# A hybrid decoder layer on one core: the last layer norm without GpSimd, four of its eight tiles finished by TensorE through a diagonal matrix

## The chip, the cores and the metric

The kernel runs on one core of a Trainium2 chip. A core has five engines that each work through a queue of their own in order: TensorE (PE; the loading of its weights is PEld), VectorE (DVE), ScalarE (ACT), GpSimd (POOL) and SyncE (SP), which here issues most of the DMA transfers. The metric is the device time of one execution in microseconds (us), and less is better.

## What is computed

One post-norm decoder layer over 1024 positions of width 1024: a token mixer in two head groups, a first layer norm, and a hierarchical mixture of experts (one of 4 groups, then 2 of its 8 experts per token). The change touches only what follows the experts, the second layer norm with its scale `ln2_g` and bias `ln2_b`:

```python
x = _layernorm(ALPHA * x + (1.0 + g2[:, None, :]) * m, ln2_g[l], ln2_b[l])

def _layernorm(x, g, b):
    mu = jnp.mean(xf, axis=-1, keepdims=True)
    var = jnp.mean(jnp.square(xf - mu), axis=-1, keepdims=True)
    y = (xf - mu) * lax.rsqrt(var + LN_EPS) * g + b
```

Everything is float32.

## The kernel before

The layer runs in stages: input projection, recurrence and gating, output projection with the first layer norm and the routing, and then the 32 experts one after the other. Each expert's result rows are added by an indirect DMA (`scatter`, line 1415) into `xad`, a table of 1024 rows in device memory that already holds `ALPHA * x`. After the last scatter has landed the **tail** begins, and all of the change lies there.

The tail works on eight tiles of 128 rows by 1024 columns. Lines 1545 and 1546 load all eight from `xad` through SP's queue; the buffers `rt` are ring buffers of the experts' weights, which the profile calls y0a, y0b, y1a and uu (two tiles each). `l2g` and `l2b`, broadcast over the 128 partitions, were loaded during the last experts (profile: vn).

`t_ops(tt)` (line 1550) returns the list of operations of tile `tt`. Two strings choose their form. `TSTAT` chooses the statistics: with "V", VectorE takes `bn_stats` over both halves (line 1556) and `bn_aggr` (1587), and ScalarE the square root (1559); with "S", ScalarE sums the row with an accumulator (1589), VectorE turns the sum into the negative mean (1590), ScalarE sums the squares around it (1591) and takes the root (1559). Then VectorE takes the reciprocal (1593), so that `sd` holds one over the deviation and `mu` the mean or its negative.

`TMODE` chooses the rest. With "F" VectorE does it in two fused operations over the tile: (r - mu) * g (line 1574), then r * sd + b (line 1572). With any other letter VectorE makes the shift in one column (1563, 1565), ScalarE normalises the tile in one pass (1598), and then come a plain multiplication by g and a plain addition of b (1570): both on GpSimd with "p", the multiplication on GpSimd and the addition on VectorE with "A", the other way round with "B". At the end SP stores the tile (1584; for tile 7 in two halves, 1582).

No scheduler orders the tail: the string `TORDER` (line 55) does, one digit for each operation, and lines 1602 and 1603 issue the next operation of that tile. As each engine takes its own instructions in that order, so do SP's stores:

```python
TSTAT = "VVVSVSVS"
TMODE = "pFBpFAFF"
TORDER = "00100102101213023231320425323423564546436567545653776777575"
...
    t_all = [t_ops(tt) for tt in range(8)]
    for tt in TORDER:
        run(t_all[int(tt)], 1)
```

So before, tiles 0 and 3 are multiplied and biased by GpSimd, tiles 2 and 5 by GpSimd and VectorE, and tiles 1, 4, 6 and 7 by VectorE alone. Also used by the change: `ident` (line 207), the 128x128 identity; `ones` (209); `eh`, made with the experts' buffers, a buffer of four 128x128 blocks that held the transposed hidden rows of an expert; and `pup`, `pup2`, `pdn` (line 1294), three PSUM buffers of two banks (profile: up, ov, dn), into which the experts' products went.

Of the kernel before, what the change touches and what calls it, by code (L numbers as in the profile page):

```python
# [15 lines left out]
AF = mybir.ActivationFunctionType  # L16
OP = mybir.AluOpType
# [6 lines left out]
P = 128  # L24
T = 1024
D = 1024
# [23 lines left out]
WE = 0  # L50
WV = ()
TB = 1
TSTAT = "VVVSVSVS"
TMODE = "pFBpFAFF"
TORDER = "00100102101213023231320425323423564546436567545653776777575"
BACC = dict(dynamic_dma_scratch_size=7168)
COLS = [slice(0, 512), slice(512, 1024)]

# [2 lines left out]
def tile_hybrid_moe_layer(  # L61
# [7 lines left out]
    nc = tc.nc  # L69
    V, S, G, PE = nc.vector, nc.scalar, nc.gpsimd, nc.tensor  # L70
# [11 lines left out]
    start = ExitStack()  # L82
# [10 lines left out]
    def cst(shape, dt, name):  # L93
        return const.tile(shape, dt, name=name)
# [112 lines left out]
    ident = cst([P, P], F32, "ident")  # L207
    V.tensor_scalar(ident, jp, 0.0, None, op0=OP.is_equal)
    ones = cst([P, P], F32, "ones")
# [36 lines left out]
    def h_turn(half, k):  # L246
        p = sm()
        for i in range(4):
            PE.transpose(p[:, i * P:(i + 1) * P], x_tile(half, k)[:, i], ident)
        return p  # L250
# [402 lines left out]
    for k in range(8):  # L653
        p = h_turn(0, k)
# [383 lines left out]
    def run(ops, m=None):  # L1038
        for _ in range(len(ops) if m is None else min(m, len(ops))):
            ops.pop(0)()  # L1040
# [205 lines left out]
    eh, eh2 = (p4.tile([P, 4, P], F32, name=n) for n in ("eh", "eh2"))  # L1246
# [47 lines left out]
    pup, pup2, pdn = (ps4.tile([P, 2, 512], F32, name=t) for t in ("up", "ov", "dn"))  # L1294
# [248 lines left out]
    l2g, l2b = l2  # L1543
# [6 lines left out]
    def t_ops(tt):  # L1550
        r, mode = rt[tt], TMODE[tt]
        mu, sd = mv8[:, tt, 0:1], mv8[:, tt, 1:2]

        def moments():
            for n, sl in enumerate(COLS):
                V.bn_stats(st8[:, tt, n], r[:, sl])

        def root(scale=1.0):
            S.activation(sd, sd, AF.Sqrt, bias=eps, scale=scale)

        def shift():
            if TSTAT[tt] == "V":
                V.scalar_tensor_tensor(mu, mu, -1.0, sd, op0=OP.mult, op1=OP.mult)
            else:
                V.tensor_tensor(mu, mu, sd, op=OP.mult)

        def part(q, sl, fused, e):
            v = (l2g, l2b)[q]
            if not fused:
                e.tensor_tensor(r[:, sl], r[:, sl], v[:, sl], op=(OP.mult, OP.add)[q])  # L1570
            elif q:
                V.scalar_tensor_tensor(r[:, sl], r[:, sl], sd, v[:, sl], op0=OP.mult, op1=OP.add)  # L1572
            else:
                V.scalar_tensor_tensor(r[:, sl], r[:, sl], mu, v[:, sl],  # L1574
                                       op0=OP.subtract if TSTAT[tt] == "V" else OP.add, op1=OP.mult)

        def both(q):
            e = {"p": (G, G), "F": (V, V), "A": (G, V), "B": (V, G), "X": (V, V), "q": (G, G)}[mode][q]
            for sl in COLS if tt == 7 else [slice(0, D)]:
                part(q, sl, mode == "F", e)  # L1580
                if q and tt == 7:
                    nc.sync.dma_start(out[0, tt * P:(tt + 1) * P, sl], r[:, sl])
            if q and tt < 7:
                nc.sync.dma_start(out[0, tt * P:(tt + 1) * P, :], r)

        if TSTAT[tt] == "V":
            ops = [moments, lambda: V.bn_aggr(mv8[:, tt], st8[:, tt]), root]
        else:
            ops = [lambda: S.activation(eyo[0], r, AF.Copy, accum_out=mu),
                   lambda: V.tensor_scalar(mu, mu, -1.0 / D, None, op0=OP.mult),  # L1590
                   lambda: S.activation(eyo[0], r, AF.Square, bias=mu, accum_out=sd),
                   lambda: root(1.0 / D)]
        ops.append(lambda: V.reciprocal(sd, sd))
        if mode == "q":
            ops.append(lambda: V.tensor_scalar(r, r, mu, sd, op0=OP.subtract if TSTAT[tt] == "V" else OP.add,
                                               op1=OP.mult))
        elif mode != "F":
            ops += [shift, lambda: S.activation(r, r, AF.Identity, bias=mu, scale=sd)]
        return ops + [lambda: both(0), lambda: both(1)]

    t_all = [t_ops(tt) for tt in range(8)]
    for tt in TORDER:
        run(t_all[int(tt)], 1)
# [23 lines left out]
```

## Time and profile before

| | |
|---|---|
| time, median of 3 runs | 1179.51 us (1179.1 to 1180.15) |
| time of the profiled execution | 1183.11 us |
| its span, first to last instruction | 1181.4 us |
| TensorE busy over the span | 88% |
| VectorE, ScalarE, GpSimd busy | 47%, 25%, 30% |
| mean granted clock of TensorE | 0.947 |

Times in the profile count from the start of the span. The granted clock is TensorE's, as a share of 2.4 GHz: it is 1.00 or 0.50 (1.2 GHz). A row of the timeline has start, duration, engine, line, operation, output and input, with the shape; "x2" are two like instructions merged, and brackets hold the idle time of the engine just before and what ended it. A row of the windows has the stretch and its length, the busy time of PE, PEld, DVE, ACT and POOL with the count of instructions in brackets, the granted clock, the share of the DMA engines that was busy and the GB/s moved. A row of the groups has line, engine, operation, output and input, shape and count, then busy us and the mean ns of one, then idle time before them.

### The profile page before, as it was taken

The page shows a single profiled execution, that of the slowest core. Times are in us where ns is not written, and L with a number is a line of the kernel's source. Part 1 is how long each engine was busy: PE and PEld are TensorE (multiplying, and loading weights), DVE is VectorE, ACT ScalarE, POOL GpSimd, SP SyncE. Part 2 cuts the span into 40 slices and gives each one's busy share as a digit, 9 for nine tenths or more (in the row PEclk, how much of TensorE's full clock was granted, in tenths as well). Part 3 has the DMA queues.
Part 4 walks back from the last instruction along what each step waited for, and adds up shares of the span by engine and source line. Part 5 has one row for each costly group of instructions (what it writes and reads, how often), then busy time and mean ns, then how long its engine had stood idle before and what let it go on. Part 6 is the DMA issues. An engine that isn't in the chain of part 4 may idle for free. (4 is left out here: it accounts for less than half of the span.)

```text
span 1181.4 us, 17353 instructions
## 1 busy us (share of the span) xinstructions
PE 1042.4 (88%) x5758; PEld 678.4 (57%) x5758; DVE 553.6 (47%) x1018; ACT 291.6 (25%) x440; POOL 359.6 (30%) x272
## 2 busy tenths in 40 slices
PE   4999999899999989998588899999998998799930
PEld 3778888788788767776333454445433553344400
DVE  6858975738664389999410211311221121211238
ACT  3363336642234442121200110101110110110113
POOL 2325643353121145552511211321141113211215
PEclk9899999999999998999799999999998998999975
DMA  9854454343211336316899979999999999999964
GB/s 278 241 164 146 143 178 144 124 157 130 89 54 54 143 143 220 120 72 248 303 393 383 351 254 371 363 386 390 371 379 395 393 371 372 394 398 384 378 247 187
DMA packets 121282, 304.55 MB, mean 258 GB/s; under 512 B 17840, under 2 KB 45144, under 8 KB 121132
## 3 DMA queue, kind: packets, MB, share of 16 engines
q1 hardware_dynamic: 111548, 275.53, 64.1%
q0 software_dynamic: 8368, 22.90, 7.2%
q10 hardware_dynamic: 1216, 4.21, 0.9%
q8 instruction: 83, 1.36, 0.5%
q14 instruction: 67, 0.55, 0.1%
HBM read 281.09 MB, written 22.88 MB: 257 GB/s over the span
## 5 line engine op out<-in xcount | busy, mean ns | idle before, releaser
L1395 DVE TENSOR_TENSOR act<-up,act 128x512 f32<-128x512 f32 x32 | 22.1, 692 | 311.6 <-ACT act L1394 234.1
L1416 POOL DMA_INDIRECT xad<-yo,tokp x36 | 52.8, 1466 | 228.4 <-DVE yo L1412 141.5
L1412 DVE SCALAR_TENSOR_TENSOR yo<-dn,wr,g2p 32x256 f32<-32x256 f32 (+2 forms) x94 | 52.1, 563 | 127.4 <-PE ov L1348 49.3
L1401 ACT ACTIVATE eh<-tp 128x512 f32<-128x512 f32 x36 | 21.1, 596 | 311.3 <-PE tp L1400 268.5
L1207 POOL DMA_INDIRECT KS<-h2d,tokp x32 | 30.5, 954 | 191.5 <-PE tp L1311 182.8
L622 PE MATMUL acc<-whi,hTh 128*128 128x512 f32 x192 | 83.0, 433 | 0.0
L166 ACT ACTIVATE whi<-wr 128x1024 fp32r<-128x1024 f32 (+1 forms) x44 | 44.9, 1021 | 128.3 <-PE acc L624 67.0
L624 PE MATMUL acc<-whi,hTl 128*128 128x512 f32 x192 | 75.9, 396 | 0.0
L623 PE MATMUL acc<-wlo,hTh 128*128 128x512 f32 x192 | 75.4, 392 | 0.0
L167 POOL TENSOR_TENSOR wlo<-wr,whi 128x1024 fp32r<-128x1024 f32 (+1 forms) x15 | 35.8, 2384 | 119.4 <-ACT whi L166 112.6
L1343 PE MATMUL up<-pring,ext 128*32 128x256 f32 (+1 forms) x564 | 53.4, 439 | 13.5 <-DMA pring<-in_w_up 10.7
L302 PEld LDWEIGHTS sm<-QP,KS 128*128 128x128 f32 x448 | 58.2, 192 | 7.3 <-issue 3.2
L618 PE MATMUL acc<-hTh,whi 128*128 128x512 f32 x144 | 59.2, 411 | 0.0
L302 PE MATMUL sm<-QP,KS 128*128 128x64 f32 x448 | 56.1, 269 | 2.6 <-DVE KS L315 1.6
L620 PE MATMUL acc<-hTh,wlo 128*128 128x512 f32 x144 | 56.9, 395 | 0.5 <-POOL wlo L167 0.2
L619 PE MATMUL acc<-hTl,whi 128*128 128x512 f32 x144 | 56.6, 393 | 0.0
L1336 PE MATMUL up<-pring,ext 128*128 128x512 f32 x128 | 56.6, 592 | 0.0
L877 PE MATMUL pa<-wh,yl 128*128 128x512 f32 (+1 forms) x128 | 51.8, 405 | 4.7 <-DVE yl L861 4.7
L876 PE MATMUL pa<-wl,yh 128*128 128x512 f32 (+1 forms) x128 | 51.6, 403 | 4.7 <-DVE wl L1048 4.7
L1394 ACT ACTIVATE act<-up 128x512 f32<-128x512 f32 x32 | 19.1, 597 | 144.4 <-PE ov L1336 52.3
L875 PE MATMUL pa<-wh,yh 128*128 128x512 f32 (+1 forms) x128 | 53.6, 419 | 1.3 <-ACT wh L1047 0.9
L443 POOL TENSOR_TENSOR vec<-vec,y1a 128x1024 f32<-128x1024 f32 x14 | 35.8, 2560 | 55.2 <-ACT y1a L442 55.2
(493 smaller groups left out, 2225.2 us busy)
## 6 DMA issues: line engine op xcount, KB each, us to landing
pring<-in_w_up SPq DMA_DIRECT2D x112, 512.0 KB
pring<-in_w_down SPq DMA_DIRECT2D x58, 512.0 KB
wr<-in_w_in SPq DMA_DIRECT2D x44, 512.0 KB
ring<-in_w_up SPq DMA_DIRECT2D x42, 512.0 KB
y1a<-in_w_ada SPq DMA_DIRECT2D x32, 512.0 KB
ring<-in_w_down SPq DMA_DIRECT2D x18, 512.0 KB
y0a<-in_w_up SPq DMA_DIRECT2D x16, 512.0 KB
y0b<-in_w_up SPq DMA_DIRECT2D x16, 512.0 KB
```

Of the source, the lines that this page charges most:

```text
L302: PE.matmul(p[:, hd], chd(KS)[:, c4, hd], chd(QP)[:, c4, hd].rearrange("p (b two i) -> p b two i", two=2, i=h)[:, :, 1, :], start=True, st ...
L618: PE.matmul(a[i], hi[:, j, sl], hTh[k], start=st, stop=False)
L619: PE.matmul(a[i], hi[:, j, sl], hTl[k], start=False, stop=False)
L620: PE.matmul(a[i], lo[:, j, sl], hTh[k], start=False, stop=sp)
L622: PE.matmul(a[i], hTh[k][:, sl], hi[:, j], start=st, stop=False)
L623: PE.matmul(a[i], hTh[k][:, sl], lo[:, j], start=False, stop=False)
L624: PE.matmul(a[i], hTl[k][:, sl], hi[:, j], start=False, stop=sp)
L875: PE.matmul(p, yh[:, k], wh[k][:, sl], start=k == 0, stop=False)
L1336: PE.matmul(p[:, h], x[:, k], gate_up(w[k], 2, h), start=k == 0, stop=k == 7)
L1343: PE.matmul(o[j * r:(j + 1) * r], x[:, k, 0:r], gate_up(w[k], m, j), start=k == 0, stop=k == 7)
L1412: V.scalar_tensor_tensor(yo[rows, n * c:(n + 1) * c], src, w[rows], g2p[rows, n * c:(n + 1) * c], op0=OP.mult, op1=OP.mult)
L1416: G.indirect_dma_start(out=xad, out_offset=bass.IndirectOffsetOnAxis(ap=tcol[rows], axis=0), in_=yo[rows], in_offset=None, bounds_check=T ...
```

## The change

`TMODE` has two forms now. For all tiles VectorE computes (r - mu) * g in one operation (`centre`). With "F" VectorE also computes r * sd + b (`finished`), as before. With "P" (tiles 0, 2, 3 and 5) ScalarE writes a 128x128 diagonal matrix, the identity times `sd` (`dg`); TensorE puts, for each half of 512 columns, first the bias into PSUM as the product of a row of ones and one row of `l2b`, and adds the product of the diagonal and the tile (`scaled`); and ScalarE copies both halves from PSUM back into the tile (`evict`), which is then stored. The statistics are by VectorE for tiles 0, 1, 3 and 7 and by ScalarE for the others, the order string is a new one, and GpSimd has nothing to do. Stores stay nine, all by SP.

```diff
-TSTAT = "VVVSVSVS"
-TMODE = "pFBpFAFF"
-TORDER = "00100102101213023231320425323423564546436567545653776777575"
+TSTAT = "VVSVSSSV"
+TMODE = "PFPPFPFF"
+TORDER = "001020010231021124152206345723246334544353425656756675367757"
...
-        def shift():
...
-        def part(q, sl, fused, e):
...
-        def both(q):
...
+        def centre(sl):
+            V.scalar_tensor_tensor(r[:, sl], r[:, sl], mu, l2g[:, sl],
+                                   op0=OP.subtract if TSTAT[tt] == "V" else OP.add, op1=OP.mult)
+
+        def store(sl):
+            nc.sync.dma_start(out[0, tt * P:(tt + 1) * P, sl], r[:, sl])
+
+
+        dg, pt = eh[:, tt % 4], (pup, pdn, pup2)[TMODE[:tt].count("P") % 3]
+
+        def scaled():
+            for n, sl in enumerate(COLS):
+                PE.matmul(pt[:, n], ones[0:1], l2b[0:1, sl], start=True, stop=False)
+                PE.matmul(pt[:, n], dg, r[:, sl], start=False, stop=True)
+
+        def evict():
+            for n, sl in enumerate(COLS):
+                S.activation(r[:, sl], pt[:, n], AF.Copy)
+            store(slice(0, D))
+
+        def finished():
             for sl in COLS if tt == 7 else [slice(0, D)]:
-                part(q, sl, mode == "F", e)
...
+                V.scalar_tensor_tensor(r[:, sl], r[:, sl], sd, l2b[:, sl], op0=OP.mult, op1=OP.add)
+                store(sl)
...
-        ops.append(lambda: V.reciprocal(sd, sd))
...
-        return ops + [lambda: both(0), lambda: both(1)]
+        ops += [lambda: V.reciprocal(sd, sd), lambda: centre(slice(0, D))]
+        if mode == "P":
+            return ops + [lambda: S.activation(dg, ident, AF.Copy, scale=sd), scaled, evict]
+        return ops + [finished]
```

## Rows read from the trace of the kernel before

**Rows 1.** Windows: the tail from 1143 on, and two single microseconds of it.
```profile
1143.00:1182.00 39.00, 0.00 (x0) 0.00 (x0) 29.85 (x42) 13.57 (x24) 17.69 (x6) 0.50 0.55 215
...
1156.00:1157.00 1.00, 0.00 (x0) 0.00 (x0) 1.00 (x1) 0.00 (x0) 0.53 (x1) 0.50 0.00 0
...
1170.00:1171.00 1.00, 0.00 (x0) 0.00 (x0) 1.00 (x3) 1.00 (x2) 0.32 (x1) 0.50 0.92 373
```

**Rows 2.** Chain of waits from 1130 on: start, duration, what.
```profile
1132.03 11.13 DMA xad<-yo,tokp
...
1167.06 2.22 DVE mv L1565
```

**Rows 3.** Timeline of VectorE: the first and the third tile's statistics.
```profile
1146.43 1.29 DVE L1556 BATCH_NORM_STATS2 st<-y0a 128x6 f32<-128x512 f32 x2 [9.71 <-DMA y0a<-xad]
...
1150.02 1.29 DVE L1556 BATCH_NORM_STATS2 st<-y0b 128x6 f32<-128x512 f32 x2 [0.64 <-DMA y0b<-xad]
```

**Rows 4.** Timeline of GpSimd, the later two of its three stretches.
```profile
1160.34 8.91 POOL L1570 TENSOR_TENSOR y0b<-y0b,vn 128x1024 f32<-128x1024 f32 x3 [3.81 <-DVE mv L1565]
1170.68 3.30 POOL L1570 TENSOR_TENSOR y1a<-y1a,vn 128x1024 f32<-128x1024 f32 x1 [1.43 <-ACT y1a L1598]
```

**Rows 5.** Timeline of VectorE from 1163.8 to 1171.8.
```profile
1163.84 3.23 DVE L1572 SCALAR_TENSOR_TENSOR y1a<-y1a,mv,vn 128x1024 f32<-128x1024 f32 x1
1166.98 2.29 DVE L1565 TENSOR_TENSOR mv<-mv 128x1 f32<-128x1 f32 x1
1169.20 1.27 DVE L1574 SCALAR_TENSOR_TENSOR uu<-uu,mv,vn 128x1024 f32<-128x1024 f32 x1
1170.39 0.14 DVE L1590 TENSOR_SCALAR mv<-mv 128x1 f32<-128x1 f32 x1
1170.50 1.28 DVE L1572 SCALAR_TENSOR_TENSOR uu<-uu,mv,vn 128x1024 f32<-128x1024 f32 x1
```

**Rows 6.** Groups by shape on VectorE in the tail: the small ones.
```profile
L1593 DVE RECIPROCAL mv<-mv 128x1 f32<-128x1 f32 x8 | 1.1, 149 | 0.6 <-ACT mv L1559 0.6
L1587 DVE BATCH_NORM_AGGREGATE mv<-st 128x2 f32<-128x12 f32 x5 | 1.0, 203 | 0.0
```

**Rows 7.** Groups by shape on ScalarE: the tail's, and an eviction of the experts.
```profile
L1559 ACT ACTIVATE mv<-mv,eps 128x1 f32<-128x1 f32 x8 | 2.2, 287 | 13.7 <-DVE mv L1587 12.5 <-DVE mv L1563 1.1
L1591 ACT ACTIVATE yo<-uu,mv 128x1024 f32<-128x1024 f32 x1 | 1.1, 1150 | 0.0
L1589 ACT ACTIVATE yo<-uu 128x1024 f32<-128x1024 f32 x1 | 1.0, 1042 | 0.0
L1591 ACT ACTIVATION_READ_ACCUMULATOR yo<-uu,mv 128x1 f32 x1 | 0.2, 187 | 0.0
...
L1401 ACT ACTIVATE eh<-tp 128x512 f32<-128x512 f32 x36 | 21.1, 596 | 311.3 <-PE tp L1400 268.5 <-PEq L1434 33.5 <-PE up L1343 9.2
```

**Rows 8.** Timeline of TensorE: full-precision matmuls of one row and of 128.
```profile
456.87 0.41 PE L945 MATMUL pl<-rb,ones 1*128 1x40 f32 x2
...
589.74 6.42 PE L1336 MATMUL up<-y0b,ext 128*128 128x512 f32 x8 [2.98 <-DVEq L1429]
595.99 3.60 PE L1336 MATMUL up<-y1a,ext 128*128 128x512 f32 x8
```

**Rows 9.** Windows: a pause of TensorE near 25 ends.
```profile
26.00:28.80 2.80, 2.74 (x9) 2.39 (x10) 1.72 (x6) 1.52 (x3) 0.00 (x0) 0.50 1.21 290
28.80:32.20 3.40, 3.40 (x10) 2.63 (x9) 3.40 (x5) 0.74 (x2) 2.26 (x2) 0.50 1.21 290
32.20:34.00 1.80, 1.80 (x11) 1.49 (x10) 0.48 (x2) 0.00 (x0) 0.00 (x0) 0.98 1.21 295
```

**Rows 10.** Timeline of SP: the last store.
```profile
1177.68 0.33 SPq L1584 DMA_DIRECT2D out<-y1a  x1
```

**Rows 11.** Windows: the last store's data.
```profile
1178.50:1179.00 0.50, 0.00 (x0) 0.00 (x0) 0.00 (x0) 0.00 (x0) 0.00 (x0) 0.50 1.03 418
...
1179.50:1180.00 0.50, 0.00 (x0) 0.00 (x0) 0.00 (x0) 0.00 (x0) 0.00 (x0) 0.50 0.56 221
```

More of the change, by code (lines that the diff above doesn't have):

```diff
@@ L1559, in root @@
             S.activation(sd, sd, AF.Sqrt, bias=eps, scale=scale)
-        def shift():
[L1562 to L1565, printed above, removed]
-        def part(q, sl, fused, e):
[L1568 to L1575, printed above, removed]
-        def both(q):
-            e = {"p": (G, G), "F": (V, V), "A": (G, V), "B": (V, G), "X": (V, V), "q": (G, G)}[mode][q]
-            for sl in COLS if tt == 7 else [slice(0, D)]:
-                part(q, sl, mode == "F", e)
[L1581 to L1584, printed above, removed]
+        def centre(sl):
[13 more added lines that the diff above has]
+        def finished():
+            for sl in COLS if tt == 7 else [slice(0, D)]:
+                V.scalar_tensor_tensor(r[:, sl], r[:, sl], sd, l2b[:, sl], op0=OP.mult, op1=OP.add)
+                store(sl)
         if TSTAT[tt] == "V":
@@ L1592, in t_ops @@
                    lambda: root(1.0 / D)]
-        ops.append(lambda: V.reciprocal(sd, sd))
[L1594 to L1598, printed above, removed]
-        return ops + [lambda: both(0), lambda: both(1)]
+        ops += [lambda: V.reciprocal(sd, sd), lambda: centre(slice(0, D))]
+        if mode == "P":
+            return ops + [lambda: S.activation(dg, ident, AF.Copy, scale=sd), scaled, evict]
+        return ops + [finished]
     t_all = [t_ops(tt) for tt in range(8)]
```

## The prediction

> **What bounds the kernel now.** I read first the windows of busy time over the tail, then the chain of waits there, then the timelines of GpSimd and VectorE, and last the prices of single instructions.
>
> The edit sits in the last 39 us, which hold no matmul at all: VectorE is busy 29.85 us in 42 instructions, GpSimd 17.69, ScalarE 13.57, and TensorE's granted clock is 0.50, its lower level of 1.2 GHz [rows 1]. The chain of waits runs through the last scatter (11.13 us), the loads of the tiles, and then almost only VectorE, a one-column operation of 2.22 us among it [rows 2]. Nothing before the loads is touched, so the start stands: first tile at VectorE at 1146.43, and a third tile at 1150.02 which VectorE had to wait for [rows 3]. By 1156 all loads have arrived: no data moves in the microsecond after [rows 1]. From the fourth tile on, tiles wait for engines.
>
> VectorE is slow because GpSimd runs beside it. While GpSimd works from 1160.34 to 1169.25, a 128x1024 scalar_tensor_tensor takes 3.23 us and one on a single column 2.29; in the gap to 1170.68 two of the same 1024-wide operations take 1.27 and 1.28 [rows 4, 5]. The gap is no quiet time otherwise: from 1170 to 1171 ScalarE is busy throughout and 373 GB/s of a store move [rows 1]. Both wide prices come from the same line pair, so only the neighbour differs.
>
> **The change, part by part.** Removed: all six GpSimd operations (17.69 us [rows 1]), the four ScalarE normalisations, the small shift operations on VectorE, and with them the contention. The six were off VectorE only on paper.
>
> *VectorE.* All eight tiles now get one 1024-wide centre-and-scale, tiles 1, 4, 6, 7 a second wide operation (tile 7 in halves); tiles 0, 1, 3, 7 have bn_stats pairs, the other four one small negation. An instruction starts about 0.08 before the stated end of the one ahead (1169.20 + 1.27 against 1170.39 [rows 5]), so a wide one costs 1.19. Sum: 11 x 1.19 + 2 halves x 0.65 (estimate: half of 1.19 and 0.06) + 4 bn_stats pairs x 1.21 (1.29 less 0.08 [rows 3]) + 4 aggregates x 0.13 + 8 reciprocals x 0.10 (203 and 149 ns less the overlap [rows 6]) + 4 negations x 0.11 [rows 5] = 13.1 + 1.3 + 4.8 + 0.5 + 0.8 + 0.4 = 21.0 us, against 29.85.
>
> *ScalarE.* Four tiles take two passes with accumulation: 1042 and 1150 ns, each with a 187 ns read of the accumulator, which I take as 1.15 + 1.20 after overlap [rows 7]; eight roots at 0.25. New is a 128x128 copy that scales the identity: not in the trace, between 0.29 (one column) and 0.60 (512 columns), estimate 0.36. Two evictions of 128x512 a tile, at 0.60 each, as the same shape out of PSUM costs elsewhere [rows 7]. Sum 9.4 + 2.0 + 1.4 + 4.8 = 17.6 us within some 23: not the bound by itself, but it is in order.
>
> *TensorE.* A full-precision 128x512 matmul shows as two records. Eight records take 3.60 us at full clock, so a matmul costs some 0.86 at 2.4 GHz; the eight before them, begun at the low clock, take 6.42 [rows 8]. At 1.2 GHz twice 0.86 is 1.71. Each of the four tiles has four: bias, product, bias, product. The one-row bias matmul with 512 columns is not in the trace. Its lower bound is the one-row matmul of 40 columns, 0.41 a pair [rows 8]; the upper is the full 0.86, which I take since it moves the same 512 columns. The first bias waits for nothing of its tile and is done during the loads. After the diagonal is ready a tile thus needs three matmuls: 2.6 us at 2.4 GHz, 5.1 at 1.2.
>
> *The clock.* TensorE stands still before the first product, so that starts at 1.2 GHz [rows 1]. What raises it: at 26.0 matmuls began again after a pause, ran nearly gapless for 6.2 us at 0.50, and from 32.2 on had 0.98 [rows 9]; and of the sixteen records from 589.74 the first eight took 6.42 us and the second eight 3.60, so the level rose within that stretch too [rows 8]. Tile 0's product, bias, product and the next tile's bias are four matmuls in a row, 6.8 us at the low level, so the clock should rise during them. The Trainium skill (TensorE: Matmul & The Clock Gate, "The HAM clock gate") says the throttled level is the default and activity releases it; the rows agree. By that the tail's first matmuls are slow and the later ones not; a matmul priced at full clock throughout would give a span of 1173.8, and at the low clock throughout 1184.1.
>
> *Laid out in the new order string*, each instruction at the time when its engine is free and its input there: VectorE 1146.46 to 1169.6 with 2.1 us of waits (0.8 for tile 2's sum from ScalarE, 1.1 for the reciprocals of tiles 3, 4 and 6). The diagonal of tile 0 is ready at 1151.6, of tile 2 at 1158.3, tile 3 at 1161.5, tile 5 at 1164.8. Its evictions queue ScalarE up: behind tile 0's second one wait tile 6's first pass, tile 2's diagonal and tile 3's root; behind tile 2's, tile 6's second pass. Every late root holds VectorE's reciprocal. Tile 5's last product ends at 1168.0 at full clock and its store is issued at 1168.7; the two halves of tile 7 follow by 1169.6. SP's queue has nine stores before and after, in the new order none stands behind a later one for more than 0.4 us. Three stores now bunch: 1 MB at some 410 GB/s is 2.6 us from 1169.6 (0.83 from issue to data, 1.5 from last data to the end, as the last store shows [rows 10, 11]) -> 1173.8. When the clock rises at 1155 this becomes 1173.9, at 1158.5 1174.7. I take 1174.2: 7.2 us less than the 1181.4 of the span.
>
> The profiled execution took 1183.11 us, 3.6 above the median 1179.51 of the runs; taking 7.2 off the median gives **1172.3** (0.6%), off the profiled time 1175.9. A measurement of this kernel can tell about 0.2%, 2.4 us, from no change.
>
> **Rivals.**
>
> 1. *TensorE stays at 1.2 GHz through the tail* (the one that ends slower). Place: the diagonal tiles' 15 matmuls behind the diagonals. For it: no row shows one-row matmuls with many columns raising the clock, and half of the new ones are such; the tail stands at 0.50 throughout. Against: it rose in both stretches [rows 8, 9]. Price: 15 x 1.71 = 25.7 us from 1151.8 with 0.8 of waits, so the last product ends at 1178.3, its evictions at 1179.0, tile 7's stores stand behind tile 5's on SP, and the span is 1184.1: 2.7 more, 1182.2. It decides if the clock has not risen by the time tile 5's first product runs, near 1170; before that VectorE or TensorE still ends ahead of the old kernel.
>
> 2. *The clock rises late*, after tile 2 or tile 3: in the same layout a rise near 1161 gives 1176.0 and near 1164 1177.7, that is 1174.1 to 1175.8 as time. The pause between tile 0's and tile 2's matmuls, some 2 to 3 us where the clock has risen early, speaks for it a little.
>
> 3. *The change does not relieve VectorE*: wide operations stay slow from ScalarE, TensorE and the stores. If four of the twelve still cost 3.2 it is 4 x 2.0 = 8 us and the time is 1180, no change. Against it: 1.27 and 1.28 were taken beside ScalarE and a store [rows 5]; nothing of TensorE's reading is in the tail's rows, which is what is left of this rival.
>
> **How the numbers follow.** Forecast 0.72 (span 1171.5 to 1175, the wait total and the unshown prices moving it by up to 2 either way), late clock 0.10, no relief 0.07, clock stays low 0.11. Faster: 0.72 + 0.10 = 0.82; same 0.07; slower 0.11. Low end 1170.3: the 2.1 us of waits on VectorE all gone. High end 1177.5: the late clock, or the wide operations at 1.5 instead of 1.19 (12 x 0.3 = 3.6) and a little of each. Outside lie rival 1, most of rival 3: under 0.2.
>
> **What would show it.** Right: no GpSimd work after the loads; 1024-wide operations on VectorE at 1.2 to 1.3 us throughout; VectorE busy near 22 us and ending near 1170; granted clock 0.50 at tile 0's product and 1.00 before tile 3's; record spacing 0.43 then; last store issued near 1169.6. Wrong: clock 0.50 past 1165, ScalarE waiting for PE over 3 us in front of evictions of tiles 3 and 5, wide operations over 1.5, or a store of tile 5 that holds tile 7's.

## The result: slower by 0.7%, on a TensorE that stayed at its low clock

The changed kernel takes 1187.92 us (median of 4 runs, 1186.19 to 1189.11) against 1179.37 for the kernel before: a ratio of 1.007 with a 95% interval of 1.0053 to 1.0088. The forecast was 1172.3, faster by 0.6%. The time lies outside its range, on the other side, and beyond the rival that was priced there (1182.2).

The profiled execution took 1188.71 us with a span of 1185.5. Its tail begins at another point than in the profile shown of before: the first load is issued at 1139.69 instead of 1143.32, because the experts ended earlier in that execution. So I compare tails, from the first load's issue to the end of the span: 38.1 us before, 45.8 after, and 30.9 in the forecast (1143.3 to 1174.2).

The windows of the changed kernel's tail, in three stages (up to the first product, the products, what follows), answer to [rows 1]:

```profile
1139.70:1148.50 8.80, 0.00 (x0) 0.00 (x0) 4.31 (x10) 1.77 (x5) 0.00 (x0) 0.50 0.90 322
1148.50:1179.30 30.80, 30.19 (x30) 7.49 (x30) 17.10 (x28) 13.51 (x31) 0.00 (x0) 0.50 0.36 147
1179.30:1185.50 6.20, 0.00 (x0) 0.00 (x0) 0.00 (x0) 1.02 (x2) 0.00 (x0) 0.50 0.44 169
```

GpSimd is idle and VectorE busy for 21.4 us, as forecast (21.0). But in the middle stage TensorE is busy for 30.2 of 30.8 us with 30 records, and its granted clock is 0.50 to the end. The forecast had 16.2 us for this stage (1151.8 to 1168.0); in the other two stages it is within half a microsecond.

The chain of waits of the changed kernel (start, duration, what) shows the same: where [rows 2] end in VectorE, it now runs, from 1157 to the last eviction, through TensorE's matmuls alone.

```profile
1157.09 2.08 PE dn L1574 x2
1159.17 2.00 PE dn L1573 x2
1161.17 2.00 PE dn L1574 x2
1163.17 2.00 PE ov L1573 x2
...
1177.20 2.02 PE up L1574 x2
...
1179.24 0.60 ACT y1a L1578
```

L1573 is the bias, L1574 the product; a matmul is two records, and the next one starts 2.00 us later. The timeline of the changed kernel has the same wide operations as [rows 5] and the last stores:

```profile
1165.86 1.28 DVE L1562 SCALAR_TENSOR_TENSOR uu<-uu,mv,vn 128x1024 f32<-128x1024 f32 x1
...
1167.18 1.28 DVE L1583 SCALAR_TENSOR_TENSOR uu<-uu,mv,vn 128x1024 f32<-128x1024 f32 x1
...
1179.24 1.09 ACT L1578 ACTIVATE y1a<-up 128x512 f32<-128x512 f32 x2 [6.93 <-PE up L1574]
1180.35 0.33 SPq L1566 DMA_DIRECT2D out<-y1a  x1
1180.77 1.21 SPq L1566 DMA_DIRECT2D out<-uu  x2
```

VectorE is relieved: 1.28 us where it took 3.2 beside GpSimd. ScalarE, however, waits 6.93 us for tile 5's last product, and tile 7's two halves, long finished, stand behind tile 5's store in SP's queue.

So two things were open: why the clock did not rise although TensorE worked almost without a gap, and why a matmul took 2.00 us where twice the full-clock price is 1.71.

### The profile page after: what moved, and what is told of

It reads as the page before. It is cut to its first block, busy times and chain, and to the rows that moved or that the text cites. A ratio compares the mean times of both kernels' runs of the same rounds, so it can differ in the third digit from the quotient of the medians.

```text
span 1185.5 us, 17424 instructions
## 1 busy us (share of the span) xinstructions
PE 1070.3 (90%) x5790; PEld 684.3 (58%) x5790; DVE 545.2 (46%) x1013; ACT 294.4 (25%) x452; POOL 341.4 (29%) x266
```

## The experiments

Three theories of the clock were set against each other: A, the one-row bias matmuls do not raise it; B, the diagonal weights, mostly zeros, do not; C, the array stands still too often while weights are loaded.

**Five stretches of matmuls behind the tail.** Each follows a pause in which ScalarE copies.

```diff
...
+    for kinds in ((one_row,), (diagonal,), (dense,), (one_row, diagonal), (dense, diagonal)):
+        for _ in range(8):
+            S.activation(eyo[0], eyo[1], AF.Copy)
+        S.activation(dia, ident, AF.Copy)
+        PE.transpose(tp()[:, 0], dia, ident)
+        for n in range(12):
+            kinds[n % len(kinds)](n)
...
```

> The changed kernel with five stretches of twelve matmuls of 128x512 behind its tail, each after a pause of some 9 us of ScalarE's copies: one-row weights alone; diagonal weights alone; dense weights alone; one-row and diagonal in turn, as in the changed kernel; dense and diagonal in turn. Theory A (one-row matmuls do not raise the clock): stretch 1 stays at 0.50 to its end, 2, 3 and 5 reach 1.00, 4 stays at 0.50. Theory B (weights that are mostly zeros do not raise it): 2 and 4 stay at 0.50, 3 reaches 1.00. Theory C (it is the time in which the array stands still while weights are loaded, 2.00 us a matmul where 1.71 would be the price): every stretch whose matmuls come 2.00 apart stays at 0.50 and every one at 1.71 rises, whatever its weights. The long total time is the added work and says nothing.

Windows of this run: one-row; diagonal before and after the rise; one-row and diagonal in turn; dense and diagonal in turn before and after the rise.

```profile
1190.00:1211.00 21.00, 20.70 (x24) 7.66 (x24) 0.00 (x0) 0.20 (x1) 0.00 (x0) 0.50 0.00 0
1220.60:1225.20 4.60, 4.60 (x7) 2.02 (x7) 0.00 (x0) 0.00 (x0) 0.00 (x0) 0.50 0.00 0
1225.20:1233.30 8.10, 8.10 (x19) 3.26 (x18) 0.00 (x0) 0.00 (x0) 0.00 (x0) 1.00 0.00 0
...
1266.70:1290.80 24.10, 24.10 (x25) 5.99 (x24) 0.00 (x0) 0.00 (x0) 0.00 (x0) 0.50 0.00 1
1300.70:1303.70 3.00, 3.00 (x5) 1.39 (x5) 0.00 (x0) 0.00 (x0) 0.00 (x0) 0.50 0.00 0
1303.70:1312.80 9.10, 8.99 (x21) 3.61 (x19) 0.00 (x0) 0.01 (x1) 0.00 (x0) 1.00 0.00 0
```

And its timeline of TensorE, first for the one-row stretch, then two matmuls each of the two mixed ones. L1607 is the one-row matmul (`1*128` are weights of one row and 128 columns), L1610 the dense and L1613 the diagonal one:

```profile
1189.86 20.84 PE L1607 MATMUL dn<-vn,ones 1*128 1x512 f32 x24
...
1266.71 2.07 PE L1607 MATMUL dn<-vn,ones 1*128 1x512 f32 x2
1268.71 2.08 PE L1613 MATMUL dn<-y0a,eh 128*128 128x512 f32 x2
...
1303.95 1.02 PE L1610 MATMUL dn<-y0a,eh 128*128 128x512 f32 x2
1304.81 1.02 PE L1613 MATMUL dn<-y0a,eh 128*128 128x512 f32 x2
```

Twelve one-row matmuls run for 20.84 us without a gap, 1.71 us apart (20.84 less 2.07 for the last, over 11), and the clock does not rise. Diagonal weights raise it within 4.6 us, so B is out. By C the one-row stretch would have risen, as its matmuls come at 1.71; it did not, so C is not the cause there. Whether the time lost between one-row and 128-row weights adds something in the mixture of the changed kernel, where both come together, no run separates. The second question is answered beside it: one-row alone comes at 1.71, dense and diagonal in turn at 0.86 at the full clock (1303.95 to 1304.81), and only one-row and 128-row weights in turn come at 2.00 (1266.71 to 1268.71).

**Does work with few rows hold a level once reached?**

```diff
...
+    for kinds in ([dense] * 10 + [rows_of_ones(1), diagonal] * 6, [dense] * 10 + [rows_of_ones(1)] * 12,
+                  [rows_of_ones(32)] * 12, [rows_of_ones(64)] * 12):
...
```

> The changed kernel with four stretches of 128x512 matmuls behind its tail, each after a pause: ten dense ones and then, without a pause, twelve in turn one-row and diagonal; ten dense and then twelve one-row; twelve of 32 rows; twelve of 64 rows. If one-row matmuls count as rest for the clock, stretch 2 falls from 1.00 to 0.50 within its one-row part and goes on at 0.50. If they only fail to raise it, stretch 2 stays at 1.00 to its end. Stretch 1 tells whether the changed kernel's own mixture keeps a level once reached. Stretches 3 and 4 tell whether it is a matter of a single row or of few rows. The long total time is the added work and says nothing.

Its windows: in stretch 2 the end of the dense part and the one-row part before and after the fall, then stretches 3 and 4.

```profile
1238.00:1244.50 6.50, 6.50 (x16) 2.65 (x14) 0.00 (x0) 0.00 (x0) 0.00 (x0) 1.00 0.00 0
1244.50:1247.30 2.80, 2.80 (x8) 1.32 (x8) 0.00 (x0) 0.00 (x0) 0.00 (x0) 1.00 0.00 0
1247.40:1262.50 15.10, 15.10 (x18) 5.23 (x16) 0.00 (x0) 0.00 (x0) 0.00 (x0) 0.50 0.00 0
1272.60:1293.40 20.80, 20.80 (x25) 7.82 (x24) 0.00 (x0) 0.00 (x0) 0.00 (x0) 0.50 0.00 1
1303.50:1324.30 20.80, 20.80 (x25) 7.85 (x24) 0.00 (x0) 0.00 (x0) 0.00 (x0) 0.50 0.00 0
```

The one-row part begins at 1.00 and the clock falls 2.9 us later without a pause: one-row matmuls alone did not hold the level either. The 32-row and the 64-row stretches stay at 0.50 too. In stretch 1 (L1615 is the diagonal, L1608 the one-row matmul) the changed kernel's own mixture, begun at 1.00 at 1203.34, fell 3.1 us in:

```profile
1204.39 1.12 PE L1615 MATMUL dn<-y0a,eh 128*128 128x512 f32 x2
1205.44 1.14 PE L1608 MATMUL dn<-vn,ones 1*128 1x512 f32 x2
1206.51 2.08 PE L1615 MATMUL dn<-y0a,eh 128*128 128x512 f32 x2
1208.51 2.07 PE L1608 MATMUL dn<-vn,ones 1*128 1x512 f32 x2
```

These rows also price the change of weights at the full clock: 1.05 us apart instead of 0.86.

**The bias by 128 rows**, an edit to the kernel that tests A in place.

```diff
+    part128 = eh2[:, 0]
+    V.memset(part128, 1.0 / P)
...
-                PE.matmul(pt[:, n], ones[0:1], l2b[0:1, sl], start=True, stop=False)
+                PE.matmul(pt[:, n], part128, l2b[:, sl], start=True, stop=False)
```

> The changed kernel with one edit: the bias goes into PSUM by a 128-row matmul of weights 1/128 instead of a one-row matmul of ones. Theory A (one-row matmuls do not raise the clock): granted clock 1.00 from the second or third diagonal tile on, time 1172 to 1177. Theory B (diagonal weights do not): clock 0.50 throughout and the time stays at 1186 to 1189. Theory C (exposed weight loads): the clock rises only if matmuls come 1.71 us apart in place of 2.00; if they stay at 2.00 it does not rise and the time stays.

1173.14 us against 1179.75, a ratio of 0.9954 (0.9939 to 0.9969); the edit turns a loss of 0.7% into a gain of 0.5%. Windows of its tail, from tile 0's first product on:

```profile
1146.20:1149.70 3.50, 3.50 (x4) 1.50 (x5) 3.46 (x5) 3.44 (x7) 0.00 (x0) 0.50 0.95 387
1149.70:1163.10 13.40, 11.63 (x27) 4.67 (x25) 12.36 (x23) 9.98 (x25) 0.00 (x0) 1.00 0.52 207
1163.10:1169.30 6.20, 0.00 (x0) 0.00 (x0) 1.18 (x2) 0.99 (x2) 0.00 (x0) 0.80 0.60 234
```

The clock rises 3.5 us after the first product, the products take 16.9 us, and the tail 31.7 (1137.65 to 1169.3). That is the forecast's own course, to within 0.8 us, in the fastest of the five runs (1171.22; the slowest took 1176.79). The edit also does away with the changes between one-row and 128-row weights, so it does not by itself tell A from C; the stretches above do, for one-row matmuls alone.

**The one-row biases early**, out of the way while the tiles are loaded.

```diff
-                PE.matmul(pt[:, n], ones[0:1], l2b[0:1, sl], start=True, stop=False)
...
+            if tt == 3:
+                biased(5)
...
+    for tt in (0, 2, 3):
+        biased(tt)
```

> The changed kernel with the six bias matmuls of tiles 0, 2 and 3 issued ahead of the tail, while the tiles are loaded, and tile 5's behind tile 3's products. Ten matmuls are left in the tail instead of sixteen. If diagonal matmuls alone do not raise the clock (theory B), or if they come 2.00 us apart and that holds it down (theory C): ten at 2.00, last product some 6 us earlier than in the changed kernel, time 1180 to 1183. Theory A: the clock rises behind tile 2's products and the time is 1173 to 1178.

1173.55, ratio 0.9956 (0.9937 to 0.9975). With only products left between the waits the clock does rise, at the end of tile 0's and again at the end of tile 2's, but it falls in between:

```profile
1151.80:1155.20 3.40, 0.59 (x2) 0.00 (x0) 2.98 (x8) 3.14 (x7) 0.00 (x0) 0.99 0.61 248
1155.30:1158.60 3.30, 3.04 (x4) 1.18 (x4) 3.17 (x6) 3.27 (x9) 0.00 (x0) 0.50 0.31 125
1158.70:1168.00 9.30, 5.91 (x13) 2.03 (x12) 7.89 (x11) 5.09 (x12) 0.00 (x0) 1.00 0.72 285
```

Its eight runs spread from 1171.04 to 1178.66; what the clock did in the slowest was not profiled.

**Bias, bias, product, product** in place of bias, product, bias, product.

```diff
                 PE.matmul(pt[:, n], ones[0:1], l2b[0:1, sl], start=True, stop=False)
+            for n, sl in enumerate(COLS):
                 PE.matmul(pt[:, n], dg, r[:, sl], start=False, stop=True)
```

> The changed kernel with the order bias, bias, product, product within a tile instead of bias, product, bias, product; weights still of one row. If the 0.29 us over 1.71 belongs to each change between one-row and 128-row weights, two matmuls of a tile come at 1.71 and two at 2.00. Should the clock stay at 0.50: the last product ends 2 us earlier, time 1185 to 1187. Should two products in a row be enough for the clock: about 1176.

1178.74, ratio 0.9983 (0.996 to 1.0005), a median between two groups: five runs from 1181.13 to 1182.09, five from 1170.3 to 1176.36. Neither branch was hit. The price of the change of weights was right: at 0.50 a pair takes 3.71 us, twice 1.71 and once 0.29:

```profile
1161.10 3.78 PE L1575 MATMUL ov<-y0b,eh 128*128 128x512 f32 x4
1164.81 3.78 PE L1573 MATMUL up<-vn,ones 1*128 1x512 f32 x4
```

In this profile, of a run of the upper group, the clock was at 1.00 for some 3.4 us and back at 0.50 from within tile 2's products on:

```profile
1152.10:1155.40 3.30, 2.50 (x6) 0.86 (x5) 2.67 (x9) 3.30 (x9) 0.00 (x0) 1.00 0.80 324
1155.60:1172.30 16.70, 16.70 (x19) 4.96 (x17) 9.81 (x14) 6.07 (x16) 0.00 (x0) 0.50 0.32 126
```

That the lower group is runs in which it stayed up longer fits the stretches above, but is argued, not shown.

**Dense filler ahead of the tail**, so that the clock is up when the tail begins.

```diff
+    for n in range(8):
+        PE.matmul(pdn[:, n % 2], ones, l2b[:, COLS[n % 2]], start=True, stop=True)
```

> The changed kernel with eight dense 128-row matmuls added on TensorE ahead of the tail, whose result nobody uses; the tail itself is unchanged, one-row biases and all. The clock is raised during the loads. If one-row matmuls only fail to raise the clock but do hold it, the tail runs at 1.00 and takes 31 to 33 us, time 1173 to 1176. If they count as rest altogether, the clock falls back in tile 0's or tile 2's matmuls and the time is 1180 to 1187.

1185.57, ratio 1.0057 (1.0036 to 1.0078).

```profile
1132.50:1137.10 4.60, 4.55 (x6) 2.01 (x7) 0.00 (x0) 0.00 (x0) 0.84 (x1) 0.50 0.16 23
1137.20:1143.90 6.70, 5.82 (x13) 2.08 (x12) 3.76 (x7) 0.29 (x1) 0.00 (x0) 1.00 0.90 311
1144.00:1145.40 1.40, 0.00 (x0) 0.00 (x0) 0.52 (x4) 1.40 (x4) 0.00 (x0) 0.52 1.02 410
1145.50:1176.00 30.50, 30.00 (x30) 7.46 (x30) 17.16 (x28) 13.41 (x30) 0.00 (x0) 0.50 0.38 151
```

The filler raised the clock after 4.6 us. It multiplies the same `ones` and the same `l2b` as the stretches of 1, 32 and 64 rows above, which did not raise it; so what differs is the number of rows, not the values. The clock then fell in the pause ahead of tile 0's product, after a one-row bias, and stayed at 0.50 through 30 us of nearly gapless mixture. This run alone cannot say whether pause or bias brought it down; stretch 1 above, where the mixture lost the level in 3.1 us, says that the mixture would have.

**All tiles on VectorE**: what does GpSimd's removal bring without TensorE?

```diff
-TMODE = "PFPPFPFF"
-TORDER = "001020010231021124152206345723246334544353425656756675367757"
+TMODE = "FFFFFFFF"
+TORDER = "0010200102312112415226345723463345443545656756676777"
```

> The changed kernel without TensorE: all eight tiles finished by VectorE's two wide operations, the order string shortened by the missing steps. If it was GpSimd that made VectorE slow: 21.0 + 4 x 1.19 = 25.8 us on VectorE and about 1 of waits, so its end lies 30 us behind the first load and the span's end 34 behind, against 38 before: 1174.5 to 1177.5, faster than before. If GpSimd's removal gains nothing by itself, 1179 or more.

1173.63, ratio 0.9948 (0.9931 to 0.9964), a little under the range expected. Its tail:

```profile
1139.00:1171.30 32.30, 0.00 (x0) 0.00 (x0) 25.72 (x41) 11.49 (x24) 0.00 (x0) 0.50 0.67 260
```

VectorE is busy 25.7 us, the tail takes 32.3. The whole gain is there without a single matmul.

**GpSimd beside it**: the same, with six wide GpSimd operations on data that nobody uses.

```diff
...
+        if step == 0:
+            G.tensor_tensor(yo2[:, 0:1], st8[:, 0, 0, 0:1], st8[:, 0, 0, 0:1], op=OP.mult)
+            for _ in range(6):
+                G.tensor_tensor(yo2, eyo[1], eyo[1], op=OP.mult)
```

> The version with all tiles on VectorE, with six 128x1024 GpSimd operations added beside it on data that nobody uses, from the first tile's statistics on. If GpSimd beside it is what makes VectorE slow, the 1024-wide operations that lie beside it take 2.9 to 3.2 us instead of 1.27, VectorE is busy some 8 us longer, time 1180 to 1183. If it is not, the time stays at 1173 to 1174.5.

1180.09, ratio 0.9998 (0.9986 to 1.0011): the gain is gone. VectorE is busy 30.9 us instead of 25.7, and the tail takes 37.5. The tail, GpSimd's work (1141.66 to 1157.72) and VectorE's timeline beside it:

```profile
1137.30:1174.80 37.50, 0.00 (x0) 0.00 (x0) 30.87 (x41) 11.37 (x24) 15.85 (x7) 0.50 0.57 224
...
1141.66 16.06 POOL L1604 TENSOR_TENSOR yo<-yo 128x1024 f32<-128x1024 f32 x6
...
1144.68 2.79 DVE L1583 SCALAR_TENSOR_TENSOR y0a<-y0a,mv,vn 128x1024 f32<-128x1024 f32 x1
...
1147.46 1.27 DVE L1556 BATCH_NORM_STATS2 st<-y0b 128x6 f32<-128x512 f32 x2
...
1148.71 1.59 DVE L1562 SCALAR_TENSOR_TENSOR y0a<-y0a,mv,vn 128x1024 f32<-128x1024 f32 x1
1150.34 2.80 DVE L1583 SCALAR_TENSOR_TENSOR y0a<-y0a,mv,vn 128x1024 f32<-128x1024 f32 x1
...
1153.13 2.83 DVE L1562 SCALAR_TENSOR_TENSOR y0b<-y0b,mv,vn 128x1024 f32<-128x1024 f32 x1
```

Three wide operations take 2.8 us, the other three that begin in this stretch 1.4 to 1.6, and bn_stats is not slowed. What decides which of them is slowed, these rows do not show. Of the 8 us expected 5.2 came, in a profile of one of the shorter runs (1176.51; the ten lie between 1176.29 and 1181.62).

**Both edits**: 128-row biases, issued early.

```diff
...
+            PE.matmul(bank_of(tt)[:, n], part128, l2b[:, sl], start=True, stop=False)
...
+    for tt in (0, 2, 3):
+        biased(tt)
```

> The changed kernel with both edits: the bias by 128-row matmuls, and those of tiles 0, 2 and 3 issued while the tiles are loaded. If the one-row weights were the cause, the clock is at 1.00 for all products but perhaps tile 0's, no run lies near 1178 as two of the runs with early one-row biases did, VectorE sets the end, tail of 30 to 31.5 us from the first load, time 1171.5 to 1173.5. If TensorE no longer limits with 128-row biases anyway, there is no difference from that kernel's 1173.1.

1172.88, ratio 0.9943 (0.9928 to 0.9958), six runs from 1171.6 to 1174.52. Against the expectation the clock was at 0.50 not only for tile 0's products but for tile 2's too, with waits of TensorE in front of both. It cost little: ScalarE waited 0.6 us for tile 2's products, and VectorE, not TensorE, ends last.

```profile
1153.65 3.78 PE L1583 MATMUL dn<-y0b,eh 128*128 128x512 f32 x4 [2.50 <-DVE st L1566]
...
ACT y0b L1589 <- PE dn L1583: 0.6, 1, 0.6
```

The time is not distinguishable from that of the version with 128-row biases in place.

**A new order for it**, with three tiles through TensorE.

```diff
-TSTAT = "VVSVSSSV"
-TMODE = "PFPPFPFF"
-TORDER = "001020010231021124152206345723246334544353425656756675367757"
+TSTAT = "VSVVSSVS"
+TMODE = "FFPPPFFF"
+TORDER = "0000101021213214233242534743656312762366476477431755447555"
...
-            for sl in COLS if tt == 7 else [slice(0, D)]:
+            for sl in COLS if tt == 5 else [slice(0, D)]:
...
+    for tt in (2, 3, 4):
+        biased(tt)
```

> The version with early 128-row biases, with new strings: tiles 2, 3 and 4 go through TensorE, the others through VectorE, statistics of tiles 0, 2, 3, 6 by VectorE, tile 5 last and in halves. The order was laid out with the durations measured here; that layout ends 1.9 us ahead of the one of the present order. So 1170.5 to 1172 if it holds; 1172.5 to 1173.5 if the stores and the start of the tail set the end.

1171.63, ratio 0.9928 (0.9909 to 0.9946): the fastest median here, faster than both kernels. Its interval overlaps that of the version before it, so the new order itself is not shown to gain. It overlaps that of all tiles on VectorE too (0.9931 to 0.9964): no run shows that TensorE gains anything beyond GpSimd's removal.

## Why the prediction was wrong

**The step that failed** is the clock: "four matmuls in a row, 6.8 us at the low level, so the clock should rise during them". Every row it rested on [rows 8, 9] was of matmuls with 128 rows; half of the new ones have one row. Measured was 0.50 through all fifteen matmuls, 30.8 us; one-row matmuls alone did not raise the clock in 20.84 us, and one-row and 128-row ones in turn not in 24.1 us. The rival that said so got 0.11. Its point for it, that no row showed one-row matmuls with many columns raising the clock, was the decisive one and should have weighed more than "it rose in both stretches", because neither stretch held such a matmul. The Trainium skill (TensorE: Matmul & The Clock Gate, "Why this matters for your kernels") asks to keep TensorE busy continuously for the full clock. Here 20.84 us of continuous one-row work stayed at 0.50, so by the measurement that alone is not sufficient.

**The size of the rival was off as well.** At 1.71 us a matmul it came to a tail of 40.8 us (1143.3 to 1184.1); measured are 45.8. The missing term is the change of weights: 15 x 0.29 = 4.4 us, of the 5.0. No row of before has one-row and 128-row weights in turn with 512 columns.

**The products' stage in figures**: 30.8 us instead of 16.2. Fifteen matmuls at 2.00 instead of 0.86 are 17.2 us more, 12.8 from the clock (15 x 0.855) and 4.4 from the weights. Of the forecast's 3.3 us of waits (16.2 less 15 x 0.86) 0.5 were left, as the others vanished behind the matmuls. 17.2 - 2.8 = 14.4, against 14.6 seen.

**What held.** VectorE's 21.0 us (21.4), the wide operation at 1.26 to 1.28 beside ScalarE, TensorE and the stores, so rival 3 fell; ScalarE's 0.36 for the diagonal (0.39 in the timeline) and 0.60 for half an eviction; the two other stages of the tail; and with the clock up the forecast's whole layout, 31.7 us for 30.9. Rival 2, the late rise, did not occur in the changed kernel.

**A loose reading that did no harm.** The forecast took GpSimd's neighbourhood for the reason why VectorE was slow from two operations "in the gap to 1170.68". Only the first lies in it: the second runs from 1170.50 to 1171.78 [rows 5], 1.1 us of it beside GpSimd's next operation [rows 4], and still takes 1.28. And not every wide operation inside GpSimd's stretch took 3.23; this one from before took about half of that:

```profile
1162.07 1.71 DVE L1574 SCALAR_TENSOR_TENSOR y1a<-y1a,mv,vn 128x1024 f32<-128x1024 f32 x1
```

So these rows did not settle the cause; the run with GpSimd's operations put back did, with the same mix of slowed and unslowed ones.

**Where the gain comes from.** The forecast gave it to the pair of edits. GpSimd's absence has all of it: 1173.63 without TensorE, 1173.14 with it and 128 rows, and 1180.09 with GpSimd's operations put back. Taking four second passes off VectorE (25.7 to 21.3 us) shortened the tail by 0.7 us only (32.34 to 31.65): of the 4.4 us VectorE lost 1.9 again in waits, and 1.8 went at the end, where the span goes on for 5.0 us behind VectorE's last operation instead of 3.2, with the last three stores issued within 1.6 us instead of 3.0.

## What to carry to other kernels

A row that shows the clock rising holds only for the kind of matmul in it: before a short stretch of matmuls is priced, look for a row with the same number of weight rows. Where a vector is already broadcast over all partitions, a 128-row matmul with weights of 1/128 cost no more than a one-row one here (1.71 us each at 0.50). Before work is moved to another engine, run the version that only removes it from the contended one: here that had all of the gain that could be told from noise, with no matmul to price.

## What the runs showed that was not expected

- Matmuls of 512 columns with 1, 32 or 64 weight rows left TensorE at 0.50 for 20.8 us of gapless work each, and one-row ones let a reached level fall after 2.9 us. Weights of 128 rows that are zero off the diagonal raised it, within 4.6 us.
- Going from one-row to 128-row weights or back costs 0.29 us at the low clock (2.00 for 1.71) and 0.19 at the full one (1.05 for 0.86); two 128-row weights in turn cost nothing extra.
- GpSimd beside VectorE slowed three of six 1024-wide operations with two tensor inputs from 1.27 to 2.8 us and the other three to 1.4 to 1.6, but not bn_stats (1.27 for a pair).
